# Norm2 in place, more expert weights ahead of the routing, and a shorter routing chain in a two-layer hybrid trunk

## The chip, the cores and the metric

The kernel runs on one core of a Trainium2 chip. The metric is the device time of one execution in microseconds; the median of three executions is compared. The names of the engines in the rows: PE is TensorE (PEld its weight loads), DVE is VectorE, ACT is ScalarE, POOL is GpSimd, and SP is the engine that issues most of the DMAs.

## The reference

Two layers work on 768 tokens of 1024 features (256 of context, 512 of the latent grid). Each layer normalises its input, projects it for four kinds of mixers, joins them, projects the result back and adds it with a gate; then it normalises again (Norm2) and sends every token to two of 32 experts. After the second layer comes a last norm.

```python
def hierarchical_moe(h, w_rg, b_rg, w_re, b_re, w_gu, w_dn):
    g_logits = hf @ w_rg.astype(jnp.float32) + b_rg.astype(jnp.float32)
    _, g_sel = lax.top_k(g_logits, 1)
    p_group = jnp.take_along_axis(jax.nn.softmax(g_logits, axis=-1), g_sel, axis=-1)
...
    w_top, i_top = lax.top_k(jax.nn.softmax(e_in_group, axis=-1), TOP_K)
    w_top = p_group * w_top / jnp.sum(w_top, axis=-1, keepdims=True)
...
    order = jnp.argsort(expert_id)
```

In the second layer only the 512 latent tokens are carried on.

## The kernel before

Tokens lie in tiles of 128 partitions: six tiles in layer 0, four in layer 1 (only the latent ones). A layer runs through its mixers, then the output projection, then the routing, then 16 pairs of experts.

**Projection and Norm2.** The columns of w_out come in four blocks of 256 (`c` = 0 to 3), each in pieces that are loaded (L1485 to L1488) and split on ACT and DVE. `evacuate` takes a tile's projection out of PSUM: tmpo (DVE, L1604), xc (DVE, L1605, which is also stored to XA in DRAM), xh, the row times Norm2's scale (POOL, L1607), and the sum of squares (ACT, L1609). PE turns xc (L1614), the copy xT is made by ACT for c < 3 and by DVE for c = 3 (L1616), and PE multiplies it with the routing weights (po). At c = 3 follow, tile by tile, ss (DVE L1628, POOL L1629 and L1630), xg, the finished Norm2 row with its features put in another order (DVE, L1636, a strided operation), its store to XG in DRAM (SP, L1638), and lg, the logits (DVE, L1639 and L1641).

**Routing.** DVE finds the group and the two experts of each token in steps of a maximum, a comparison and an index: r_m, r_eq, r_ix, r_pen, Ms (L1713 to L1742). The masks go to PE as Am (L1745); from PE's running counts come code, then one-hot rows yes (L1793), and PE multiplies these with MV, which holds token numbers and weights by expert (`by_kind`, L1773, writes it). Out comes row (L1800), the list of tokens of each expert. The softmax weights (r_ex, r_zs, pg, e, gw, gp) and the counts cnt run on DVE between these steps. POOL then gathers rows of XG by the list (L1827, `rows`); PE turns the gathered rows (pt, L1907) and runs the experts.

**Weights of the experts.** A layer has 96 pieces of 1 MB: two of gate and up and one of down for each expert (in_moe_w_gu, in_moe_w_dn). They go through a ring of 18 slots:

```python
SLOTS = ((2, 2, 14), (2, 2, 14))
EARLY = (6, 6)
DEEP = 4
...
        wpre = SLOTS[L][0] + SLOTS[L][1] - PRE
```

The three numbers of a layer are the slots in three pools of memory. The slots of the first two (4) are filled while the projection runs, six more (EARLY) are loaded when the XG writes have been issued, and the rest when the first gather has gone out (`mark`), with at most DEEP = 4 loads under way. SP's queue keeps its order. Between the ring's last piece and the next, SP reads 17 counts (cnti) into registers. From then on a piece is loaded when a pair has used up the one in its slot.

**Norms.** norm1 squares a tile on ACT (L468), makes 1/sqrt by a logarithm and an exponential (L291, L292, with a table load L190), scales the tile on DVE (L476) and lets PE turn it (L487). The last norm does the same without the turn (L2051, L2059).

Of the kernel before, what the change touches and what calls it, by code (L numbers as in the profile page):

```python
# [2095 lines left out]
```

## Time and profile before

| what | value |
|---|---|
| runs | 1787.74, 1791.43, 1797.10 us; median 1791.43 |
| the profiled execution | 1788.17 us, span 1786.4 us, granted TensorE clock 0.928 |
| busy share of the span | PE 83%, DVE 40%, ACT 29%, POOL 20% |
| moved by DMA | 365.87 MB, mean 205 GB/s |

The span is the time from the first instruction to the last; the execution's own time has 1.8 us more around it. The shares are means over stages of very different kinds (mixers, projection, experts), so a stage has to be read by itself. PE takes part in nearly everything; DMA is busy in stretches.

### The profile page before, as it was taken

How to read it: one execution, taken by the hardware profiler on the slowest of the kernel's cores; microseconds unless marked ns; L12 is line 12 of the kernel's file. 1: busy time of each engine (PE TensorE's matmuls, PEld its weight loads, DVE VectorE, ACT ScalarE, POOL GpSimd, SP SyncE). 2: the span in 40 equal slices, each digit the busy share in tenths (PEclk: the TensorE clock that was granted, in tenths of full speed). 3: DMA queues.
4: the chain of work that ended last, by engine and by line, in shares of the span. 5: the costliest groups of instructions: out<-in, count | busy, mean ns of one | idle time of the engine just before them, and what ended most of it. 6: DMA issues, size and time to landing. Idle time of an engine off the chain costs nothing. (4 is left out here: it accounts for less than half of the span.)

```text
span 1786.4 us, 26530 instructions
## 1 busy us (share of the span) xinstructions
PE 1479.2 (83%) x10467; PEld 989.5 (55%) x10467; DVE 709.6 (40%) x1423; ACT 523.5 (29%) x1064; POOL 364.0 (20%) x271
## 2 busy tenths in 40 slices
PE   5999999989889748878885989998787766878783
PEld 3888778746679723322324978676465762322221
DVE  5353353485733561111114352635875262111111
ACT  5242452464423100000004432625643211000001
POOL 0012120120102334635431030301200132111100
PEclk9999989999999869999997999989898888999997
DMA  8342411167447399899994332202443659999994
GB/s 269 107 137 70 123 55 33 36 225 233 145 160 210 118 385 334 303 388 382 371 318 140 92 90 70 73 30 72 145 160 112 182 193 378 376 368 369 380 388 173
DMA packets 182864, 365.87 MB, mean 205 GB/s; under 512 B 42705, under 2 KB 93569, under 8 KB 182401
## 3 DMA queue, kind: packets, MB, share of 16 engines
q1 hardware_dynamic: 172368, 342.11, 54.1%
q0 software_dynamic: 9216, 20.99, 4.7%
q8 instruction: 130, 2.13, 0.5%
q14 instruction: 78, 0.63, 0.1%
q10 hardware_dynamic: 1072, 0.01, 0.0%
HBM read 338.48 MB, written 39.65 MB: 212 GB/s over the span
## 5 line engine op out<-in xcount | busy, mean ns | idle before, releaser
L288 PE MATMUL mm<-w,xT 128*64 128x512 f32 x1072 | 287.5, 624 | 22.5 <-PEq L1993 11.6
L288 PE MATMUL pj<-h,w 128*128 128x256 f32 (+1 forms) x1224 | 227.2, 341 | 0.5 <-DVE u L932 0.3
L288 PEld LDWEIGHTS pj<-h,w 128*128 128x128 f32 x1224 | 189.0, 191 | 28.8 <-issue 5.2
L288 PEld LDWEIGHTS mm<-w,xT 128*64 128x64 f32 x1072 | 88.4, 143 | 189.1 <-issue 158.3
L288 PE MATMUL sc<-w,aT 128*64 128x512 f32 x536 | 136.9, 600 | 18.7 <-ACT aT L1933 17.2
L1923 ACT ACTIVATE ac<-mm 128x256 f32<-128x256 f32 (+1 forms) x35 | 13.4, 383 | 358.0 <-PE mm L288 358.0
L288 PE MATMUL pj<-w,h 128*128 128x256 f32 x864 | 118.1, 294 | 0.0
L1924 DVE TENSOR_TENSOR ac<-ac,mm 128x256 f32<-128x256 f32 (+1 forms) x35 | 14.7, 421 | 253.5 <-ACT ac L1923 253.5
L288 PEld LDWEIGHTS pj<-w,h 128*128 128x128 f32 x864 | 111.3, 199 | 3.8 <-issue 3.1
L1971 POOL DMA_INDIRECT XA<-yes,row x32 | 50.8, 1589 | 300.6 <-DVEq L1993 270.9
L288 PEld LDWEIGHTS sc<-w,aT 128*64 128x64 f32 x536 | 44.4, 136 | 88.3 <-issue 57.2
L288 PE MATMUL mm<-w,h 128*128 128x256 f32 x624 | 83.5, 294 | 11.6 <-PEq L1511 6.4
L518 DVE TENSOR_TENSOR w<-w 128x2048 fp32r<-128x2048 f32 (+1 forms) x26 | 58.0, 2231 | 81.6 <-ACT w L516 81.6
L288 PEld LDWEIGHTS mm<-w,h 128*128 128x128 f32 x624 | 80.2, 201 | 12.2 <-issue 6.6
L1907 PE MATMUL pt<-masks,w 128*128 128x128 f32 x256 | 44.2, 308 | 43.7 <-PEq L1993 25.7
L1907 PEld LDWEIGHTS pt<-masks,w 128*128 128x128 f32 x256 | 30.5, 154 | 89.0 <-issue 77.1
L288 PE MATMUL sc<-h 128*128 128x256 f32 (+3 forms) x144 | 62.2, 551 | 10.7 <-ACT um L1208 9.9
L1607 POOL TENSOR_TENSOR xh<-xc,gr 128x512 f32<-128x512 f32 (+1 forms) x25 | 30.9, 1237 | 195.4 <-DVE xc L1605 132.6
L1954 POOL TENSOR_SCALAR yes<-gate,own 128x1024 f32<-128x1024 f32 (+1 forms) x19 | 60.8, 3199 | 16.9 <-DMA w<-XG,row 13.5
L1908 ACT COPY xT<-pt 128x512 f32<-128x512 f32 x32 | 18.7, 585 | 155.2 <-PE pt L1907 135.7
L516 ACT ACTIVATE w<-w 128x2048 fp32r<-128x2048 f32 (+1 forms) x26 | 48.0, 1848 | 50.7 <-PE pj L288 36.7
L288 PE MATMUL x<-u 64*32 64x32 f32 (+5 forms) x944 | 54.4, 250 | 8.4 <-DVE u L772 8.0
(391 smaller groups left out, 2420.7 us busy)
## 6 DMA issues: line engine op xcount, KB each, us to landing
w<-in_moe_w_gu_dram SPq DMA_DIRECT2D x128, 1024.0 KB
w<-in_moe_w_dn_dram SPq DMA_DIRECT2D x64, 1024.0 KB
w<-in_w_mod_dram SPq DMA_DIRECT2D x40, 1024.0 KB
w<-in_w_in_dram SPq DMA_DIRECT2D x22, 1024.0 KB
wm<-in_w_mod_dram SPq DMA_DIRECT2D x8, 1024.0 KB
XG<-xg SPq DMA_DIRECT2D x10, 512.0 KB
w<-in_w_out_dram SPq DMA_DIRECT2D x8, 512.0 KB
w<-in_w_out_dram SPq DMA_DIRECT2D x16, 256.0 KB
```

The lines of the kernel that those rows point to most:

```text
L288: TE.matmul(o, lhsT, rhs, start=start, stop=stop, **kw)
L516: S.activation(hi[:, :, 0:o], raw[:, :, 0:o], AF.Copy)
L518: V.tensor_tensor(lo[:, :, 0:o], raw[:, :, 0:o], hi[:, :, 0:o].bitcast(F32), op=ALU.subtract)
L1607: G.tensor_tensor(xh[:, t0 - qt0:t0 - qt0 + m, cs], xs, bc(gr[:, 1, w], 0, m), op=ALU.mult)
L1907: TE.transpose(pt[:, u * P:(u + 1) * P], xg[:, o:o + P], ident)
L1908: (V.tensor_copy if g else S.copy)(xT[:, 4 * g:4 * g + 4], pt.rearrange("p (k t) -> p k t", k=4))
L1923: S.activation(ac[rs_], pm[rs_, 0:256], AF.Silu)
L1924: V.tensor_tensor(ac[rs_], ac[rs_], pm[rs_, 256:512], op=ALU.mult)
L1954: G.tensor_scalar(gt[rs_], gate[rs_, 1], own[rs_], None, op0=ALU.mult)
L1971: G.indirect_dma_start(out=XA, out_offset=bass.IndirectOffsetOnAxis(ap=row, axis=0), in_=ye, in_offset=None, bounds_check=T - 1, oob_is_er ...
```

## The change

- **Norm2 in place.** POOL writes xh in the order of features in which XG is read (the write has a stride), the shift row is stored in that order in DRAM by the modulation, and DVE finishes the row in xh itself, without strides and without xg. XG is written from xh. xT is copied by ACT for all c.
- **Slots.** Still 18 per layer, but 7 (layer 0) and 9 (layer 1) in the first two pools instead of 4. So 7 and 9 pieces are loaded during the projection, then six as before, then 5 and 3.
- **Routing.** The routing's tiles (the pool "rout") are opened after the projection's pools are closed. Mp and the first products of MV go from DVE to POOL; the subtraction of gate from POOL to DVE. That subtraction, the weights and the counts are issued only after row. PE's products for the weights and for the second list of rows go behind the first half of pair 0.
- **Norms.** norm1 multiplies by a diagonal (dgn) on PE instead of scaling the tile and turning it; in the branch that runs this concerns layer 1. The table loads are issued ahead of the first square.

```diff
 RING, RING2 = 5, 5
-SLOTS = ((2, 2, 14), (2, 2, 14))
+SLOTS = ((2, 5, 11), (2, 7, 9))
...
                 V.tensor_copy(AB2s[L][:, :, g // 2 - 3, 4 * (g % 2):4 * (g % 2) + 4],
                               pm[:, 0:P].rearrange("p (j c) -> p c j", j=4)[:, 0:2, :])
             if g >= 4:
-                for w in range(2):
+                if g in (6, 7):
+                    mp = cp.tile([P, P], F32, name="mp", tag="mp", bufs=1)
+                    V.tensor_copy(mp.rearrange("p (e q) -> p q e", e=2), mr.rearrange("p (q e) -> p q e", e=2))
+                    for w in range(2):
+                        nc.sync.dma_start(MOD[L][w, 3 * D:4 * D].rearrange("(e i j q) -> i j e q", e=2, i=2, j=4)[g - 6],
+                                          mp.rearrange("(j r) (e q) -> j r e q", r=32, e=2)[:, w])
+                for w in range(2) if g not in (6, 7) else ():
                     nc.sync.dma_start(MOD[L][w, cs].rearrange("(j c) -> j c", j=4),
                                       mr.rearrange("(j r) c -> j r c", r=32)[:, w, :])
...
-                if L and then and n == 0:
-                    ln_exp()
                 rstd_of(ss, ss, D)
+            dgs = {}
+
             def scale(n):
-                x_, ss = sss.pop(n)
-                V.tensor_scalar(xn[n], x_, ss, None, op0=ALU.mult)
+                _, ss = sss.pop(n)
+                dgs[n] = wk.tile([P, P], F32, name="dgn", tag="dgn", bufs=3)
+                V.tensor_scalar(dgs[n], ident, ss, None, op0=ALU.mult)
...
-                        TE.transpose(pt[:, (n - n0) * P:(n - n0 + 1) * P], xn[n][:, k * P:(k + 1) * P], ident)
+                        mm(pt[:, (n - n0) * P:(n - n0 + 1) * P], xn[n][:, k * P:(k + 1) * P], dgs[n], True, True, skip_group_check=True)
...
+            if L and then:
+                ln_exp()
             staged(range(NT), fetch, square, scale, turn)
...
-        wr_ = pr.pool("rout")
...
-        lg = wr_.tile([P, N, 36], F32, name="lg")
+        lg = tabp.tile([P, N, 36], F32, name="lg")
...
-            G.tensor_tensor(xh[:, t0 - qt0:t0 - qt0 + m, cs], xs, bc(gr[:, 1, w], 0, m), op=ALU.mult)
+            pairs = "p n (q e) -> p n q e"
+            G.tensor_tensor(xh[:, t0 - qt0:t0 - qt0 + m].rearrange("p n (e c q) -> p c n q e", e=2, c=4)[:, c],
+                            xs.rearrange(pairs, e=2), bc(gr[:, 1, w], 0, m).rearrange(pairs, e=2), op=ALU.mult)
...
-            (S.copy if c < 3 else V.tensor_copy)(xT[:, 0:m], pt[:, 0:m * 2 * P].rearrange("p (u k t) -> p u k t", u=m, k=2))
+            S.copy(xT[:, 0:m], pt[:, 0:m * 2 * P].rearrange("p (u k t) -> p u k t", u=m, k=2))
...
-                xg = wk.tile([P, D], F32, name="xg", tag="xg", bufs=2)
-                pairs = "p (q e) -> p q e"
-                V.scalar_tensor_tensor(xg.rearrange("p (e q) -> p q e", e=2), xh[:, n - qt0].rearrange(pairs, e=2), ss[:, n:n + 1],
-                                       shift[:, w].rearrange(pairs, e=2), op0=ALU.mult, op1=ALU.add)
-                nc.sync.dma_start(XG[n * P:(n + 1) * P, :], xg)
+                V.scalar_tensor_tensor(xh[:, n - qt0], xh[:, n - qt0], ss[:, n:n + 1], shift[:, w], op0=ALU.mult, op1=ALU.add)
+                nc.sync.dma_start(XG[n * P:(n + 1) * P, :], xh[:, n - qt0])
...
         ph.close()
         ro.close()
         u1.close()
+        wr_ = pr.pool("rout")
         wpools[2] = ew.pool("moew2", side="right")
         yes = wpools[2].tile([P, YE, D], F32, name="yes")
...
             G.memset(t_, 0.0)
         for w in ws:
             row_bcast(gate[:, w], MOD[L][w, 5 * D:6 * D])
-        if not last:
-            G.tensor_tensor(gate[:, 1], gate[:, 1], gate[:, 0], op=ALU.subtract)
         prefetch(EARLY[L])
...
-        V.tensor_tensor(Mp, Ms[:, :, :, 0:16], Ms[:, :, :, 16:32], op=ALU.add)
...
-        by_kind(V, 0, [bc(tok1[:, i, q_], 0, 2) for i in range(2)])
+        G.tensor_tensor(Mp, Ms[:, :, :, 0:16], Ms[:, :, :, 16:32], op=ALU.add)
+        by_kind(G, 0, [bc(tok1[:, i, q_], 0, 2) for i in range(2)])
+        known = []
...
-            V.scalar_tensor_tensor(row, val[:, 0], -1.0, val[:, 1], op0=ALU.add, op1=ALU.add)
+            known.append(V.scalar_tensor_tensor(row, val[:, 0], -1.0, val[:, 1], op0=ALU.add, op1=ALU.add))
...
+        with tc.issue_after(known[0].ins):
+            if not last:
+                V.tensor_tensor(gate[:, 1], gate[:, 1], gate[:, 0], op=ALU.subtract)
+            ex = sm([4], "ex4")
...
+            by_kind(V, 2, in_parts(V, gw, "gp"))
+            V.tensor_scalar(e1, e1, 1873.0, None, op0=ALU.add)
+            V.tensor_copy(cnti, cnt[0:1, 0])
-        slot_weights(ohs, tabs[0])
...
-        def block_in(xg, xT=None):
+        def block_in(xg, xT=None, engs=(S.copy, V.tensor_copy)):
...
-                (V.tensor_copy if g else S.copy)(xT[:, 4 * g:4 * g + 4], pt.rearrange("p (k t) -> p k t", k=4))
+                engs[g](xT[:, 4 * g:4 * g + 4], pt.rearrange("p (k t) -> p k t", k=4))
...
-        slot_weights(slot_table(wk, 1, tabs[1]["row"]), tabs[1])
-        xT = into(0)
+        xT = block_in(xgs[0], None, (S.copy, S.copy))
+            if p_ == 0:
+                slot_weights(ohs, tabs[0])
+                slot_weights(slot_table(wk, 1, tabs[1]["row"]), tabs[1])
...
-        if n == 2:
-            ln_exp()
...
+    ln_exp()
     staged(range(2, NT), square, scale)
```

How the change moves instructions is seen best in the order of each engine. SP in layer 1's projection, from the c = 2 block on; before (rows carry the waits, DMAHW a load or store queue, DMASW a gather queue):

```order
L1450 DMA w_25458<-in_moe_w_gu_dram 128x2x1024 [waits DMAHW2_49]
L1488 DMA w<-in_w_out_dram 128x4x256 [waits DMAHW4_49,DMAHW5_49,DMAHW3_49,DVE_49]
L1555 DMA xc<-XA 128x4x256 [waits DMAHW7_49,DMAHW6_49,PE_49]
L1606 DMA XA<-xc 128x2x256 x2
L306 DMA gr<-MOD_103 128x256 [waits Pool_49]
L306 DMA gr<-MOD_103 128x256 [waits DMAHW0_49]
L1485 DMA w<-in_w_out_dram 128x2x256 [waits DMAHW3_49,DMAHW1_49,DVE_49]
L1486 DMA w<-in_w_out_dram 128x2x256 [waits DMAHW2_49]
L1555 DMA xc<-XA 128x4x256 [waits DMAHW6_49,DMAHW5_49,PE_49]
```

One load of expert weights stands ahead of two pieces of w_out, and none between them. The same stretch of SP now:

```order
L1460 DMA w_25487<-in_moe_w_gu_dram 128x2x1024 [waits DMASW6_49,DMASW4_49,DMAHW2_49,DMASW0_49,PE_49]
L1498 DMA w<-in_w_out_dram 128x4x256 [waits DMAHW4_49,DMAHW5_49,DMAHW3_49,DVE_49]
L1564 DMA xc<-XA 128x4x256 [waits DMAHW7_49,DMAHW6_49,PE_49]
L1465 DMA w_25543<-in_moe_w_dn_dram 128x2x1024
L1495 DMA w<-in_w_out_dram 128x2x256 [waits DMAHW3_49,DVE_49]
L1496 DMA w<-in_w_out_dram 128x2x256
L1615 DMA XA<-xc 128x2x256 [waits DMAHW0_49]
L1615 DMA XA<-xc 128x2x256 [waits DMAHW1_49]
L306 DMA gr<-MOD_103 128x256 [waits DMAHW2_49,Pool_49]
L306 DMA gr<-MOD_103 128x256
L1465 DMA w_25643<-in_moe_w_dn_dram 128x2x1024 [waits DMAHW4_49]
L1564 DMA xc<-XA 128x4x256 [waits DMAHW1_49,DMAHW5_49,DMAHW0_49,PE_49]
```

Two loads of down pieces have come in, one of them right ahead of w_out; three more of gate and up follow within five rows. The load that was there before now waits for PE and three gather queues besides the one queue.

DVE in layer 0 where Norm2 ends and the routing begins; before:

```order
L1713 TENSOR_REDUCE r_m_11853<-lg 128x4 [waits DVE_49]
L1605 TENSOR_TENSOR xc<-xc,tmpo 128x256 [waits DVE_49]
L1636 SCALAR_TENSOR_TENSOR xg<-xh,ss,shift 128x512x2 [waits DMAHW0_49,Pool_49]
L1639 TENSOR_TENSOR lg<-po,ss 128x36 [waits PE_49]
L1616 COPY xT<-pt 128x256 [waits PE_49]
L1641 TENSOR_TENSOR lg<-lg,wb_10849 128x36 [waits DVE_49]
L1628 TENSOR_REDUCE ss<-ssq 128x1 [waits Activation_49]
L1714 TENSOR_TENSOR r_eq_11847<-lg,r_m_11853 128x16
L1715 TENSOR_TENSOR r_eq_11847<-r_eq_11847,iom 128x16 [waits DVE_49]
L1636 SCALAR_TENSOR_TENSOR xg<-xh,ss,shift 128x512x2 [waits DMAHW3_49,Pool_49]
L1639 TENSOR_TENSOR lg<-po,ss 128x36 [waits PE_49]
L1716 TENSOR_REDUCE r_ix<-r_eq_11847 128x4 [waits DVE_49]
```

Steps of the routing (r_m, r_eq, r_ix) stand between the last tiles, and each xg waits for the store of the one before last. The same place of DVE now:

```order
L1646 SCALAR_TENSOR_TENSOR xh<-xh,ss,shift 128x1024 [waits Pool_49]
L1648 TENSOR_TENSOR lg<-po,ss 128x36 [waits PE_49]
L1640 TENSOR_REDUCE ss<-ssq 128x1 [waits Activation_49]
L1650 TENSOR_TENSOR lg<-lg,wb_10862 128x36 [waits DVE_49]
L1646 SCALAR_TENSOR_TENSOR xh<-xh,ss,shift 128x1024 [waits Pool_49]
L1648 TENSOR_TENSOR lg<-po,ss 128x36 [waits PE_49]
L1650 TENSOR_TENSOR lg<-lg,wb_10862 128x36 [waits DVE_49]
L1721 TENSOR_REDUCE r_m_11868<-lg 128x4 [waits DMAHW4_49,DMAHW6_49,DMAHW2_49,DMAHW7_49,DMAHW1_49,DMAHW0_49]
L1721 TENSOR_REDUCE r_m_11868<-lg 128x2 [waits DVE_49]
L1722 TENSOR_TENSOR r_eq_11862<-lg,r_m_11868 128x16 [waits DVE_49]
```

The steps of the routing now all stand behind the last lg, and the first of them waits for six DMA queues. xg has become xh, and the xT copy is gone from DVE.

DVE in layer 0 from the last Am on; before:

```order
L1745 TENSOR_TENSOR Am<-Ms 128x64 [waits DVE_49]
L1755 TENSOR_TENSOR Mp<-Ms 128x192
L1864 RECIPROCAL r_zs<-r_zs 128x6 [waits DVE_49]
L1773 TENSOR_TENSOR MV<-Mp,tok_94 128x192 [waits DVE_49]
L1759 COPY cn<-mm 128x32 [waits PE_49]
L1773 TENSOR_TENSOR MV<-Mp,tok_94 128x192
L1762 TENSOR_SCALAR mo<-cn 128x16 [waits DVE_49]
L1762 TENSOR_SCALAR mo<-cn 128x16
L1866 TENSOR_TENSOR e_11972<-e_11972,r_zs 128x12 [waits Activation_49]
L1882 TENSOR_TENSOR cnt<-cn 128x16
L1885 TENSOR_SCALAR cnt<-cn 128x16
L1867 TENSOR_TENSOR r_zs<-e_11972 128x6 [waits DVE_49]
```

Steps of the weights (r_zs, e) and counts (cnt) stand among those that lead to code. The same place of DVE now, up to row and the gate subtraction:

```order
L1753 TENSOR_TENSOR Am<-Ms 128x64 [waits DVE_49]
L1766 COPY cn<-mm 128x32 [waits PE_49]
L1769 TENSOR_SCALAR mo<-cn 128x16 [waits DVE_49]
L1769 TENSOR_SCALAR mo<-cn 128x16
L1774 TENSOR_TENSOR e_11931<-mm,mo 128x192 [waits DVE_49,Activation_49]
L1781 SCALAR_TENSOR_TENSOR u__11932<-e_11931,u__11932 128x192 [waits DVE_49]
L1782 TENSOR_TENSOR tm_11925<-Ms,u__11932 128x384 [waits DVE_49]
L1783 TENSOR_REDUCE code<-tm_11925 128x12 [waits DVE_49]
L1803 TENSOR_TENSOR yes<-iota_84,code 128x768 [waits DVE_49]
L1803 TENSOR_TENSOR yes<-iota_84,code 128x768
...
L1810 SCALAR_TENSOR_TENSOR row_11944<-val 128x16 [waits DVE_49]
L1863 TENSOR_TENSOR gate<-gate 128x1024 [waits DMAHW3_49,DMAHW2_49]
```

Mp, MV, r_zs, e of the weights and cnt have left the stretch; gate stands behind row, and everything else of the weights behind gate.

## Rows read from the trace of the kernel before

**Rows 1.** Page, slices: DMA share in 40 equal parts of the span, in tenths.

```profile
DMA  8342411167447399899994332202443659999994
```

**Rows 2.** Windows, layer 1: span, busy us of each engine, clock, DMA share, GB/s.

```profile
1420.00:1440.00 20.00, 20.00 (x173) 20.00 (x173) 7.33 (x10) 6.40 (x17) 5.55 (x4) 1.00 0.90 248
1440.00:1460.00 20.00, 15.72 (x126) 14.97 (x124) 11.41 (x21) 4.28 (x13) 6.61 (x10) 0.93 0.32 118
...
1470.00:1490.00 20.00, 7.39 (x56) 4.32 (x57) 10.62 (x62) 2.38 (x4) 4.39 (x6) 0.55 1.03 410
...
1600.00:1700.00 100.00, 79.33 (x314) 27.69 (x316) 13.91 (x22) 7.29 (x16) 14.73 (x11) 0.95 1.01 374
```

**Rows 3.** Windows, layer 0, in the expert stage.

```profile
715.00:723.00 8.00, 6.26 (x18) 1.87 (x18) 2.00 (x4) 0.64 (x2) 3.89 (x2) 1.00 0.07 24
...
735.00:917.00 182.00, 150.18 (x628) 52.96 (x626) 27.92 (x43) 14.68 (x33) 86.23 (x42) 0.98 1.03 380
```

**Rows 4.** Timeline of SP, layer 1: start, us issuing, and what.

```profile
1451.79 0.33 SPq L1638 DMA_DIRECT2D XG<-xg  x1
...
1465.86 1.29 SPq L1455 DMA_DIRECT2D w<-in_moe_w_dn_dram  x2
...
1498.43 3.40 SPq L1455 DMA_DIRECT2D w<-in_moe_w_dn_dram  x2
1512.08 4.16 SPq L1450 DMA_DIRECT2D w<-in_moe_w_gu_dram  x4
```

**Rows 5.** Timeline of DVE, layer 0: first and last tile of c = 3.

```profile
600.90 2.07 DVE L1636 SCALAR_TENSOR_TENSOR xg<-xh,ss,shift 128x1024 f32<-128x1024 f32 x1 [0.97 <-POOL ss L1630]
602.81 0.41 DVE L1616 COPY xT<-pt 128x256 f32<-128x256 f32 x1
...
623.26 2.00 DVE L1636 SCALAR_TENSOR_TENSOR xg<-xh,ss,shift 128x1024 f32<-128x1024 f32 x1 [0.65 <-POOL ss L1630]
```

**Rows 6.** Timeline of DVE, layer 1: first and last tile of c = 3.

```profile
1449.69 2.07 DVE L1636 SCALAR_TENSOR_TENSOR xg<-xh,ss,shift 128x1024 f32<-128x1024 f32 x1 [0.97 <-POOL ss L1630]
...
1462.94 2.01 DVE L1636 SCALAR_TENSOR_TENSOR xg<-xh,ss,shift 128x1024 f32<-128x1024 f32 x1 [0.68 <-POOL ss L1630]
```

**Rows 7.** DMA view of 1440 to 1475 us: GB/s in 40 slices.

```profile
GB/s 331 361 267 66 0 0 0 0 0 150 19 0 0 9 253 366 280 0 0 0 0 332 267 0 295 370 84 0 0 220 346 220 257 206 365 412 426 426 403 440
```

**Rows 8.** Timelines of DVE and ACT in the last norm.

```profile
1776.15 1.28 DVE L2059 SCALAR_TENSOR_TENSOR o<-x,ss,gf 128x1024 f32<-128x1024 f32 x1 [13.70 <-ACT ss L292]
...
1774.29 1.28 ACT L190 ACT_TABLE_LOAD   x1
```

**Rows 9.** Timeline of DVE, layer 0: from the last Am to row.

```profile
631.33 0.22 DVE L1745 TENSOR_TENSOR Am<-Ms 128x64 bf16<-128x64 f32 x1
...
632.82 2.35 DVE L1885 TENSOR_SCALAR cnt<-cn 128x16 f32<-128x16 f32 x1
...
641.41 0.16 DVE L1800 SCALAR_TENSOR_TENSOR row<-val 128x16 int32<-128x16 f32 x1
```

**Rows 10.** Timeline of POOL, layer 0, the same stretch.

```profile
632.69 2.45 POOL L1698 TENSOR_TENSOR gate<-gate 128x1024 f32<-128x1024 f32 x1 [1.25 <-DMA gate<-MOD]
642.49 1.28 POOL L1827 DMA_INDIRECT w<-XG,row  x1 [7.35 <-DMA w<-in_moe_w_gu_dram]
```

**Rows 11.** Timeline of PE, layer 0: products for weights, and pair 0.

```profile
641.64 0.80 PE L288 MATMUL mm<-MV,yes 128*128 128x64 bf16 x12 [2.10 <-DVE row L1800]
...
663.27 0.44 PE L1931 MATMUL po<-masks,ac 128*128 128x128 f32 x2 [1.26 <-DVE ac L1924]
```

**Rows 12.** Timeline of PE, layer 1: first half of pair 0.

```profile
1486.86 7.65 PE L288 MATMUL mm<-w,xT 128*64 128x512 f32 x32
```

**Rows 13.** Timeline of ACT, norm1 of layer 1.

```profile
961.16 1.28 ACT L190 ACT_TABLE_LOAD   x1
```

**Rows 14.** Groups of PE, by form: busy us and mean ns of one.

```profile
L288 PE MATMUL x<-u 128*128 128x128 f32 x80 | 12.8, 289 | 0.0
...
L1614 PE MATMUL pt<-masks,xc 128*128 128x128 f32 x80 | 15.3, 303 | 3.7 <-DVE lg L1639 3.7
```

More of the change, by code (lines that the diff above doesn't have):

```diff
@@ L1849, in layer @@
             rows(p_)
-        ex = sm([4], "ex4")
-        pg = sm([1], "pg")
-        V.tensor_tensor(ex, gl, m0.to_broadcast([P, N, 4]), op=ALU.subtract)
-        S.activation(ex, ex, AF.Exp)
-        V.tensor_reduce(pg, ex, axis=AX.X, op=ALU.add)
-        e2 = wr_.tile([P, 2, N], F32, name="e2")
-        zs = sm([1], "zs")
-        V.tensor_tensor(le2, le, m1.to_broadcast([P, N, 32]), op=ALU.subtract)
-        S.activation(le2, le2, AF.Exp)
-        V.tensor_reduce(zs, le2, axis=AX.X, op=ALU.add)
@@ L1861, in layer @@
-        V.tensor_tensor(m2, m2, m1, op=ALU.subtract)
-        S.activation(e2[:, 1], m2.rearrange("p n o -> p (n o)"), AF.Exp)
-        V.memset(e2[:, 0], 1.0)
-        V.reciprocal(zs, zs)
-        V.reciprocal(pg, pg)
-        V.tensor_tensor(e2, e2, bc(zs.rearrange("p n o -> p (n o)"), 0, 2), op=ALU.mult)
-        V.tensor_tensor(zs.rearrange("p n o -> p (n o)"), e2[:, 0], e2[:, 1], op=ALU.add)
-        V.reciprocal(zs, zs)
-        V.tensor_tensor(zs, zs, pg, op=ALU.mult)
-        gw = wr_.tile([P, 2, N], F32, name="gw")
@@ L1871, in layer @@
-        V.tensor_tensor(gw, e2, bc(zs.rearrange("p n o -> p (n o)"), 0, 2), op=ALU.mult)
-        by_kind(V, 2, in_parts(V, gw, "gp"))
-        slot_weights(ohs, tabs[0])
-        V.tensor_scalar(e1, e1, 1873.0, None, op0=ALU.add)
-        V.tensor_tensor(tm2, Ms, bc(e1, 0, 2), op=ALU.mult)
-        V.tensor_reduce(left, tm2.rearrange("p r n (h a) -> p r n h a", h=2), axis=AX.X, op=ALU.add)
-        V.tensor_scalar(left, left, -2000.0, None, op0=ALU.add)
-        cnt = wr_.tile([P, 2, 17], F32, name="cnt")
@@ L1889, in layer @@
-        V.tensor_scalar(cnt[:, 0, 16:17], cnt[:, 0, 16:17], -128.0, 0.0, op0=ALU.add, op1=ALU.max)
-        cnti = tabp.tile([1, 17], I32, name="cnti")
-        V.tensor_copy(cnti, cnt[0:1, 0])
+        with tc.issue_after(known[0].ins):
+            if not last:
+                V.tensor_tensor(gate[:, 1], gate[:, 1], gate[:, 0], op=ALU.subtract)
+            ex = sm([4], "ex4")
+            pg = sm([1], "pg")
+            V.tensor_tensor(ex, gl, m0.to_broadcast([P, N, 4]), op=ALU.subtract)
+            S.activation(ex, ex, AF.Exp)
+            V.tensor_reduce(pg, ex, axis=AX.X, op=ALU.add)
+            e2 = wr_.tile([P, 2, N], F32, name="e2")
+            zs = sm([1], "zs")
+            V.tensor_tensor(le2, le, m1.to_broadcast([P, N, 32]), op=ALU.subtract)
+            S.activation(le2, le2, AF.Exp)
+            V.tensor_reduce(zs, le2, axis=AX.X, op=ALU.add)
+            V.tensor_tensor(m2, m2, m1, op=ALU.subtract)
+            S.activation(e2[:, 1], m2.rearrange("p n o -> p (n o)"), AF.Exp)
+            V.memset(e2[:, 0], 1.0)
+            V.reciprocal(zs, zs)
+            V.reciprocal(pg, pg)
+            V.tensor_tensor(e2, e2, bc(zs.rearrange("p n o -> p (n o)"), 0, 2), op=ALU.mult)
+            V.tensor_tensor(zs.rearrange("p n o -> p (n o)"), e2[:, 0], e2[:, 1], op=ALU.add)
+            V.reciprocal(zs, zs)
+            V.tensor_tensor(zs, zs, pg, op=ALU.mult)
+            gw = wr_.tile([P, 2, N], F32, name="gw")
+            V.tensor_tensor(gw, e2, bc(zs.rearrange("p n o -> p (n o)"), 0, 2), op=ALU.mult)
+            by_kind(V, 2, in_parts(V, gw, "gp"))
+            V.tensor_scalar(e1, e1, 1873.0, None, op0=ALU.add)
+            V.tensor_tensor(tm2, Ms, bc(e1, 0, 2), op=ALU.mult)
+            V.tensor_reduce(left, tm2.rearrange("p r n (h a) -> p r n h a", h=2), axis=AX.X, op=ALU.add)
+            V.tensor_scalar(left, left, -2000.0, None, op0=ALU.add)
+            cnt = wr_.tile([P, 2, 17], F32, name="cnt")
+            c0_, c1_ = cnt[:, 0, 0:16], cnt[:, 1, 0:16]
+            V.tensor_tensor(c1_, cn[:, 0:16], cn[:, 16:32], op=ALU.add)
+            V.tensor_scalar(c1_, c1_, 128.0, 4.0, op0=ALU.is_gt, op1=ALU.mult)
+            V.scalar_tensor_tensor(c1_, cn[:, 0:16], 64.0, c1_, op0=ALU.is_gt, op1=ALU.add)
+            V.tensor_scalar(c0_, cn[:, 16:32], 64.0, 2.0, op0=ALU.is_gt, op1=ALU.mult)
+            V.tensor_tensor(c0_, c0_, c1_, op=ALU.add)
+            V.tensor_tensor(cn, cn, mo, op=ALU.add)
+            V.tensor_reduce(cnt[:, 0, 16:17], cn, axis=AX.X, op=ALU.max)
+            V.tensor_scalar(cnt[:, 0, 16:17], cnt[:, 0, 16:17], -128.0, 0.0, op0=ALU.add, op1=ALU.max)
+            cnti = tabp.tile([1, 17], I32, name="cnti")
+            V.tensor_copy(cnti, cnt[0:1, 0])
```

8 lines of the change are left out of this document (removed).

## The prediction, made before the changed kernel ran

> **What bounds the kernel now.** I read the page's slices first, then tables by stage, then timelines at the joints. In the slices [rows 1] the DMA digits reach 9 only in two long stretches, the expert stages of the two layers. By stage, layer 1 from 1600 to 1700 us [rows 2] has the DMA engines busy 1.01 of the time, PE 79 of 100 us: there the weight stream, 96 pieces of 1 MB, sets the pace. It is fed from a ring of 18 slots, so the stream's end is set by when it starts and how much was loaded before. The same table shows room ahead of it: from 1440 to 1460 us the share is 0.32 (13.6 of 20 us idle). Layer 0 differs [rows 3]: from 715 to 723 us the share is 0.07 while PE works, so the ring is full and PE is late; only from 735 on is DMA the bound (1.03). In layer 0 what counts is therefore when PE gets its first rows; in layer 1 when the stream can run. The page's sums (PE 83%) mix both and decide nothing.
>
> SP's timeline of layer 1 [rows 4] gives the second joint: the six early pieces start at 1465.86, right behind the last XG write at 1464.97; the ring's last two are issued by 1498.43 + 3.40 = 1501.83; piece 18 only at 1512.08. In the 10.25 us between, SP's program reads the 17 counts into registers.
>
> **Edit 1, Norm2 in place (both layers).** Per tile DVE ran a strided xg of 2.00 to 2.07 us [rows 5, 6]; the new one is contiguous, 128x1024, and the nearest row is the final norm's op of the same kind and size, 1.28 us [rows 8]. Going by that row, the tile's round in the new DVE order is: a small reduction of about 0.2 (Am, 128x64, takes 0.22 [rows 9]), the way over POOL 0.97 (the idle time ahead of the xg at 600.90), 1.28, and lg twice plus tmpo, about 0.8 (an estimate: two of 0.2 and one of the 0.41 of a 128x256 operation; xc runs during POOL's way). That is 3.2 us. Layer 0, six tiles: the first still starts at 600.90, the sixth at 600.90 + 5 x 3.2 = 616.9, end 618.2 against 623.26 + 2.00 = 625.26: -7.1. Layer 1, four tiles: from 1449.69, end 1449.69 + 3 x 3.2 + 1.28 = 1460.6 against 1464.95: -4.4. The xT copies that leave DVE (0.41 each, [rows 5]) are in this. POOL's xh now writes with a stride, which no row of before shows; bounds are no dearer (nothing) and DVE's own ratio of strided to contiguous, 2.00/1.28 = 1.56, on some 0.7 us (+0.4 a tile, +2 in layer 0 if all lay on the path). I take nothing, because POOL's xh runs under DVE's 1.28 and the lg work.
>
> **Edit 2, the tiles of the routing come from memory that the projection frees.** The order shows that the first r_m now waits on six DMA queues: all XG writes must have landed. Before, the last write was hidden behind the routing. Its price is bounded by the GB/s slices [rows 7], 0.875 us each: behind the issue at 1451.79 [rows 4] bytes move until the 17th slice ends at 1454.9, so at most 3.1 us. r_m starts at 618.2 + 0.1 + 3.1 = 621.4 in layer 0 and about 1463.8 in layer 1. From the end of the last xg to the start of the last Am passed 631.33 - 625.26 = 6.1 us [rows 5, 9], in which the routing's 36 steps shared DVE with the last lg and with steps of the weights. The weights' steps go, the few routing steps that had been done before come in: 5.4 us, an estimate between 5 and 6. Am then starts at 626.8 instead of 631.33.
>
> **Edit 3, the chain from Am to row.** Before, 641.41 - 631.33 = 10.1 us [rows 9]. In it a 128x16 cnt operation takes 2.35 us; POOL's gate subtraction (2.45 us, [rows 10]) covers the same time from 632.69. Both leave the chain: gate goes behind row, cnt too. Some fifteen more operations of the weights, about 0.1 us each, go behind row as well. 10.1 - 2.2 - 1.8 = 6.1 us. Row at 632.9, gather 1.1 later as before (642.49 - 641.41), 634.0 against 642.49: **-8.5 us**. Mp and two MV products move to POOL. Their cost there is unknown: nothing if they end during DVE's code and yes work, at most 1.4 us if four POOL operations of 0.35 us each hold DVE. I take nothing, since PE needs MV only after yes. The row shows the two engines standing on each other (2.35 under 2.45). [...]
>
> The weights' small matmuls (36 in layer 0, three runs of 12, the longest 0.80 us [rows 11], together at most 2.4) move behind pair 0's first half. There PE waits 1.26 us for ac [rows 11], which covers part: at most +1.1, I take 0.8. Layer 0 in all: **-7.7**, bounds -3.5 (landing 5 us, POOL and contention in full) and -11. Since PE and the full ring hold until 723, then DMA from a full ring, the shift passes through to the layer's end whole; the three extra preloads of layer 0 give nothing by themselves.
>
> **Edit 4, nine pieces instead of four before the routing in layer 1.** Five pieces leave the stretch that begins with the early loads. At 406 GB/s (1470 to 1490 shows 410, [rows 2]) one takes 2.6 us: -13.0. The stretch itself starts 4.4 us sooner (edit 1). SP then reaches piece 18 at 1512.08 - 17.4 = 1494.7. The slot it takes is free when pair 0's first half ends, 1486.86 + 7.65 = 1494.5 before [rows 12], some 3 earlier after. So SP still sets the time, and the stream, and with it the end, move by **-17.4**. Bounds: -20 if the counts' reading shrinks into the wait, -4.4 if the five pieces only fill time in which something else was waited for. Their cost where they go: 13 us of DMA in 1420 to 1460, where 2 and 13.6 us are idle [rows 2]; w_out's pieces could come up to 2.6 us late. Nothing taken.
>
> **Edit 5, small ones.** Two table loads of 1.28 us [rows 8, 13] go into idle time of ACT ahead of the norms: -2.6. In norm1 of layer 1 the scale becomes a 128x128 diagonal and transposes become products: 48 transposes before, 48 products after. Rows: 128x128 f32 products 289 ns, transposes 303 ns [rows 14]: nothing. [...]
>
> **Sum.** 1788.2 (span 1786.4 and 1.8 around it) - 7.7 - 17.4 - 2.6 = 1760.5. The median of the runs, 1791.4, is 3.3 above that execution, so I give 1761.
>
> **Rivals.**
> A. Layer 1's preloads don't count: something other than SP and DMA (memory of the new slots free late) sets piece 18. Against it stands the idle DMA before 1460; for it, that order puts more waits on the loads. Only -4.4 is left of edit 4: 1774.
> B. The routing gains nothing: the landing takes 8 us instead of 3 since early pieces and gate follow at once, and POOL's strided writes stretch each tile. Edits 1 to 3 fall to nothing in layer 0 (+7.7) and the start of the stretch in layer 1 (+4.4): 1773.
> C. The change doesn't do what it says: the stream in both layers is bound by its total of bytes and the gaps reappear elsewhere (a later idle DMA as in 715 to 723). What is left are the table loads and a few us: 1783.
> D. Slower: a preload that waits for its memory holds the queue. SP issues in order, and behind the new loads stand w_out pieces, xc and XA writes of the projection. If one holds SP until a stage of the projection ends, PE waits for w_out. It decides against the change from 14 us a layer (28 in all); at 20 us a layer the time is 1761 + 40 = 1801. For it: in the order one of layer 1's loads now waits for PE and three gather queues where it waited for one load. Against it: the idle DMA time from 1440 to 1460 says that the projection leaves room for loads that come late.
> [...]
>
> **Chances.** Forecast 0.62, A 0.13, B 0.10, C 0.07, D 0.06, E 0.02. The forecast alone spans 1745 (all upper bounds) to 1770. The range must take A and B in and leaves C, D, E out: 1745 to 1777. A difference under 0.5% (9 us) can hardly be told from none; faster are forecast, A and B, 0.85; same C, 0.07; slower D and E, 0.08.
>
> **What would show it.** Right: xh of 1.3 us per tile, the rounds 3.2 us apart; r_m 3 us behind the last XG issue; row about 6 us behind Am; gather of layer 0 near 634; piece 18 of layer 1 some 26 us sooner than 1512 (17.4, and 7.7 and 1.3 won before it), DMA share near 1 from there on; no table load between square and ss in the last norm. Wrong: waits of PE on w_out in the projection (D); an idle gap of DMA between pieces 17 and 18 of more than 5 us (A); r_m more than 5 us behind the last write or POOL's xh over 1.1 us (B); a final shift of the stream's end that is smaller than that of its start (C).

## The result, and the profile after

The kernel became slower: 1800.43 us median against 1787.29, ratio 1.0066, 95% interval [1.0048, 1.0083]; the forecast was 1761. Each kernel ran 20 times for this comparison. The profiled execution has a span of 1795.5 us against 1786.4. One experiment below (e10) runs in 1768.76 us, ratio 0.9892 [0.9863, 0.9921]. It keeps most of the change, takes back what made it slow, and adds two things that the change did not have: counts read one at a time, which alone make the kernel before 0.9945 of its time (e9), and eight small products on PE (e7).

Cutting both spans at the same seven events shows where it went. All columns are us, differences of starts in one profiled execution each, so a row adds up to its span. e1 to e11 are the experiments below. a: start to the last product of PE that reads um, a tile of layer 0's mixers. b: to the projection's first product. c: to pair 0's first product. d: to the first square of norm1 in layer 1. e: to the first product of layer 1's projection. f: to pair 0's first product there. g: to the end.

| kernel | a | b | c | d | e | f | g |
|---|---|---|---|---|---|---|---|
| before | 516.2 | 5.5 | 131.0 | 307.3 | 429.4 | 97.5 | 299.5 |
| after | 519.1 | 8.8 | 124.9 | 311.3 | 437.3 | 97.5 | 296.6 |
| e1 | 518.7 | 11.2 | 126.2 | 309.6 | 432.3 | 98.3 | 288.3 |
| e2 | 515.1 | 5.4 | 130.7 | 307.2 | 436.4 | 97.6 | 306.0 |
| e3 | 517.6 | 11.0 | 124.8 | 309.0 | 428.2 | 99.1 | 289.9 |
| e4 | 511.8 | 10.5 | 127.5 | 307.7 | 430.5 | 95.7 | 297.1 |
| e6 | 515.9 | 10.9 | 125.1 | 308.5 | 433.2 | 99.1 | 285.5 |
| e7 | 514.8 | 5.5 | 127.5 | 308.2 | 430.2 | 98.8 | 286.2 |
| e8 | 513.8 | 9.6 | 121.7 | 309.7 | 433.5 | 96.6 | 292.2 |
| e9 | 511.2 | 5.6 | 130.8 | 300.7 | 429.2 | 97.1 | 293.9 |
| e10 | 518.5 | 5.6 | 123.6 | 305.3 | 433.5 | 96.6 | 284.9 |
| e11 | 515.0 | 5.5 | 124.1 | 304.8 | 433.5 | 93.7 | 294.5 |

Column a scatters by 8 us between kernels that barely differ there (e3 and e4 are the same up to it), column e by 5 among those without the added table loads, and column g by 4 between e3, e6 and e7, whose programs are the same there; so no cause is read from a few us in these three. From before to after: a +2.9 (scatter), b +3.2, c -6.1, d +4.0, e +7.9, f 0, g -2.9; the sum is +9.1. Part of the predicted gain in layer 0 is there (c), but b takes half of it back and d more than the other half: b, c and d together take 443.8 us before and 445.0 after. The largest loss (e, with norm1 of layer 1) and the smallness of the gain in g (with the last norm) hang on the table loads, which follow first.

**ACT in the last norm** (timeline: start, us, line, operation), against the one load of [rows 8]. Before, the first square on ACT and the last operation of the norm on DVE:

```profile
1773.12 1.06 ACT L2051 ACTIVATE o<-x 128x1024 f32<-128x1024 f32 x1 [15.22 <-DMA x<-XA]
...
1781.44 1.28 DVE L2059 SCALAR_TENSOR_TENSOR o<-x,ss,gf 128x1024 f32<-128x1024 f32 x1 [0.32 <-ACT ss L292]
```

After, ACT:

```profile
1757.10 1.28 ACT L190 ACT_TABLE_LOAD   x1
1772.49 1.28 ACT L2066 ACT_TABLE_LOAD   x1 [14.10 <-DMA x<-XA]
...
1774.95 1.28 ACT L291 ACT_TABLE_LOAD   x1
1776.24 0.29 ACT L291 ACTIVATE ss<-ss,eps 128x1 f32<-128x1 f32 x1
1776.56 1.28 ACT L292 ACT_TABLE_LOAD   x1
1777.85 0.20 ACT L292 ACTIVATE ss<-ss 128x1 f32<-128x1 f32 x1
...
1779.11 1.28 ACT L291 ACT_TABLE_LOAD   x1
1780.40 0.29 ACT L291 ACTIVATE ss<-ss,eps 128x1 f32<-128x1 f32 x1
1780.72 1.28 ACT L292 ACT_TABLE_LOAD   x1
```

L190 is the load ahead that the change moved. It runs at 1757.10, right behind the last pair; then a conditional follows (L2022), the norm's first square loads again (L2066), and from there every Ln (L291) and every Exp (L292) of the four tiles has a load of its own. VectorE's four norm operations show the price:

```profile
1778.08 1.28 DVE L2072 SCALAR_TENSOR_TENSOR o<-x,ss,gf 128x1024 f32<-128x1024 f32 x1 [16.45 <-ACT ss L292]
...
1790.57 1.28 DVE L2072 SCALAR_TENSOR_TENSOR o<-x,ss,gf 128x1024 f32<-128x1024 f32 x1 [2.88 <-ACT ss L292]
```

They stand (1790.57 - 1778.08) / 3 = 4.16 us apart. From the moment the first x is there to the last of them it took 1790.57 - 1772.49 = 18.1 us, before 1781.44 - 1773.12 = 8.3: +9.8. In norm1 of layer 1 the same, against [rows 13]:

```profile
965.22 1.28 ACT L291 ACT_TABLE_LOAD   x1
966.52 0.29 ACT L291 ACTIVATE ss<-ss,eps 128x1 f32<-128x1 f32 x1
...
967.87 1.28 ACT L292 ACT_TABLE_LOAD   x1
...
969.38 1.28 ACT L291 ACT_TABLE_LOAD   x1
...
970.99 1.28 ACT L292 ACT_TABLE_LOAD   x1
...
974.30 1.28 ACT L190 ACT_TABLE_LOAD   x1
```

Here the load that should have been ahead runs behind the first two tiles, and they load four times. From norm1's first square to the last product that turns a tile it took 30.4 us before and 38.8 after; 31.8 in e1, which has one load there again.

**The diagonal in norm1.** The instructions of PE that turn the six tiles of layer 1 (count, then ns min/median/max, first and last start), before and after:

```profile
L487 PE MATMUL mm<-masks,xn x48: 270/273/477, 964.8 to 990.4; 128*128 128x128 f32 x48
```

```profile
L288 PE MATMUL mm<-dgn,xn x96: 273/275/582, 969.8 to 1002.9; 128*128 128x128 f32 x96
```

Each of the 48 products is two matmuls of PE, each as long as one transpose. Little of this shows in the time: the stretch of 30.4 us above became 31.5 to 31.8 us in the kernels with the diagonal and one table load there.

**The weight loads of the next layer.** SP issues the first w_in pieces of layer 1 at 956.70, before at 932.93:

```profile
932.93 1.88 SPq L511 DMA_DIRECT2D w<-in_w_in_dram  x3
```

```profile
956.70 1.86 SPq L521 DMA_DIRECT2D w<-in_w_in_dram  x3
```

**Layer 0's tail and routing**, against [rows 5, 9] (DVE) and [rows 10] (POOL):

```profile
606.96 1.28 DVE L1646 SCALAR_TENSOR_TENSOR xh<-xh,ss,shift 128x1024 f32<-128x1024 f32 x1 [0.97 <-POOL ss L1642]
...
611.92 1.29 DVE L1646 SCALAR_TENSOR_TENSOR xh<-xh,ss,shift 128x1024 f32<-128x1024 f32 x1 [1.60 <-POOL ss L1642]
...
614.86 1.74 DVE L1646 SCALAR_TENSOR_TENSOR xh<-xh,ss,shift 128x1024 f32<-128x1024 f32 x1 [0.71 <-POOL ss L1642]
...
624.94 1.28 DVE L1646 SCALAR_TENSOR_TENSOR xh<-xh,ss,shift 128x1024 f32<-128x1024 f32 x1 [0.78 <-POOL ss L1642]
...
629.72 0.24 DVE L1721 TENSOR_REDUCE r_m<-lg 128x4 f32<-128x16 f32 x2 [3.16 <-DMA XG<-xh]
...
641.88 0.18 DVE L1810 SCALAR_TENSOR_TENSOR row<-val 128x16 int32<-128x16 f32 x1
```

```profile
614.79 0.73 POOL L1618 TENSOR_TENSOR xh<-xc,gr 128x256 f32<-128x256 f32 x1
...
642.36 1.98 POOL L1837 DMA_INDIRECT w<-XG,row  x1 [5.60 <-DVE row L1810]
```

Each in-place operation takes 1.28 us, or 1.74 where POOL's xh runs beside it (614.79 and 614.86); the rounds are (624.94 - 606.96) / 5 = 3.6 us apart on average, and the first is the longest (611.92 - 606.96 = 4.96 us); r_m waits 3.16 us for the XG writes.

**PE at the start of layer 0's projection** (weight loads):

```profile
524.67 0.28 PEld L288 LDWEIGHTS mm<-w,h 128*128 128x128 f32 x1 [5.53 <-ACTq L1521]
527.87 2.43 PEld L288 LDWEIGHTS mm<-w,h 128*128 128x128 f32 x11 [2.91 <-issue]
```

One weight load, then 2.91 us without a wait on anything that the profile shows ("issue").

**Layer 1's stream**, windows against [rows 2], then SP and PE against [rows 4, 12]:

```profile
1440.00:1460.00 20.00, 20.00 (x173) 20.00 (x172) 5.55 (x7) 5.08 (x13) 2.61 (x2) 1.00 0.84 289
...
1480.00:1500.00 20.00, 4.12 (x28) 2.87 (x29) 12.54 (x77) 2.73 (x8) 5.67 (x9) 0.50 1.02 402
1500.00:1520.00 20.00, 18.88 (x108) 7.23 (x108) 3.88 (x16) 2.19 (x4) 2.79 (x3) 0.97 0.67 242
1600.00:1700.00 100.00, 82.95 (x337) 28.57 (x335) 16.29 (x25) 8.04 (x18) 15.76 (x12) 0.97 1.01 372
```

```profile
1473.18 2.72 SPq L1647 DMA_DIRECT2D XG<-xh  x2
...
1492.07 3.58 SPq L1465 DMA_DIRECT2D w<-in_moe_w_dn_dram  x2
1513.81 2.27 SPq L1460 DMA_DIRECT2D w<-in_moe_w_gu_dram  x4
```

```profile
1498.88 8.18 PE L288 MATMUL mm<-w,xT 128*64 128x512 f32 x32
...
1510.02 3.65 PE L288 MATMUL sc<-w,aT 128*64 128x512 f32 x16 [0.46 <-ACT aT L1946]
```

Piece 18 is issued at 1513.81, 0.14 us behind the end of pair 0 (1510.02 + 3.65 = 1513.67), and the DMA engines idle a third of 1500 to 1520 us.

### The profile page after: what moved, and what is told of

It reads as the page before. It is cut to its first block, busy times and chain, and to the rows that moved or that the text cites. A ratio compares the mean times of both kernels' runs of the same rounds, so it can differ in the third digit from the quotient of the medians.

```text
span 1795.5 us, 26666 instructions
## 1 busy us (share of the span) xinstructions
PE 1479.9 (82%) x10515; PEld 999.4 (56%) x10515; DVE 696.1 (39%) x1410; ACT 546.3 (30%) x1089; POOL 361.4 (20%) x276
## 3 DMA queue, kind: packets, MB, share of 16 engines
q8 instruction: 131, 2.15, 0.5%
## 5 line engine op out<-in xcount | busy, mean ns | idle before, releaser
L288 PE MATMUL x<-u 64*32 64x32 f32 (+5 forms) x944 | 54.7, 251 | 11.2 <-DVE u L782 9.3
```

The source lines that it names most:

```text
L288: TE.matmul(o, lhsT, rhs, start=start, stop=stop, **kw)
```

## The experiments

Ratios are to the kernel before, run on the same chip beside it. The times given are medians; a difference by the ratios and one by the medians can be 2 us apart. e1 to e4 ran on one chip, e6 to e11 on another.

**e1_tables_back**: the changed kernel with the two table loads where they were.

```
 S.activation(junk, x_, AF.Square, accum_out=ss)
+if L and then and n == 0:
+    ln_exp()
...
-if L and then:
-    ln_exp()
 staged(range(NT), fetch, square, scale, turn)
...
 fixed(S.activation(o_, xt, AF.Square, accum_out=ss))
+if n == 2:
+    ln_exp()
...
-ln_exp()
 staged(range(2, NT), square, scale)
```

> The changed kernel with the two table loads issued where they were before the change, nothing else undone. Theory T (the loads ahead of the norms are not kept: ACT changes its table for each logarithm and each exponential, 5 loads in norm1 of layer 1 and 9 in the last norm instead of 1 and 1): 15 us less than the changed kernel (5.4 in norm1, 9.8 in the last norm), about 1785 us, ratio to the kernel before 0.999. Rival R (the loss sits in Norm2, the routing or the slots, and the table loads were moved at a gain of 2.6 us): 1803 us, ratio 1.008 or more.

Measured: 1786.4 us, 0.9986 [0.9967, 1.0005], not told apart from the kernel before. One load in each norm again:

```profile
1772.86 1.28 ACT L190 ACT_TABLE_LOAD   x1
1774.16 0.29 ACT L291 ACTIVATE ss<-ss,eps 128x1 f32<-128x1 f32 x1
1774.49 0.20 ACT L292 ACTIVATE ss<-ss 128x1 f32<-128x1 f32 x1
```

1800.4 - 1786.4 = 14 us were the loads (theory T).

**e2_tables_alone**: the kernel before with the same lines moved the other way, and nothing else.

> The kernel before with the move of the two table loads alone. Theory T: 14 to 15 us slower than the kernel before, ratio 1.008, with four table loads between the first square and the third in norm1 of layer 1 and two per tile in the last norm; pairs of the last layer may load tables too. Rival R: 2.6 us faster, ratio 0.9985.

Measured: 1799.4 us, 1.0064 [1.0037, 1.009]: this edit alone loses about 12 us, nearly as much as the whole change. Its excess stands in columns e (+7.0) and g (+6.5); T had 14 to 15.

**e3_l0_slots_back**: e1 with layer 0's three added preloads taken back.

```
-SLOTS = ((2, 5, 11), (2, 7, 9))
+SLOTS = ((2, 2, 14), (2, 7, 9))
```

> Table loads back as in the first run, and layer 0's slots back to 2, 2, 14, layer 1's kept at 2, 7, 9. Theory W (layer 0's larger second pool lies on the memory into which the next layer's first w_in pieces were loaded during the experts, so that these now wait for the last scatters): w_in issued near 933 us again, norm1 4 to 6 us earlier than in the first run, about 1780 us, ratio 0.996. Rival (w_in is late for another reason, or norm1 waits for its tokens anyway): within 1 us of the first run.

Measured: 1780.66 us, 0.9955 [0.9933, 0.9977]. w_in is issued 23 us sooner than in e1 (959.36 there), column e is 4.1 shorter, the time 5.7:

```profile
936.11 1.74 SPq L521 DMA_DIRECT2D w<-in_w_in_dram  x3
```

**e4_slots_back**: e1 with both layers' slots as before, `SLOTS = ((2, 2, 14), (2, 2, 14))`.

> Table loads back and the slots of both layers back to 2, 2, 14: Norm2 in place, the routing and the diagonal alone. Theory G (with nine pieces loaded ahead, piece 18 waits for the end of pair 0, not for SP): with the old slots piece 18 again goes out when SP has read the counts, so the preloads of layer 1 are worth the difference of the two gates, 6 us and not 13: 1786 us, ratio 0.999. Rival (the forecast's sum): 13 us above the third run.

Measured: 1785.2 us, 0.9992 [0.9967, 1.0018], not told apart from the kernel before. Against e3, layer 1's five preloads are worth 4.5 us (6.6 by the ratios), not 13: column g is 7.2 shorter with them, column f 3.4 longer. As G said, piece 18 goes out here as soon as the last count is read (at 1506.57), 8 us behind the end of pair 0 (1498.95):

```profile
1506.93 4.19 SPq L1460 DMA_DIRECT2D w<-in_moe_w_gu_dram  x4
```

**e6_shift_store_back**: e3 with the shift row stored in plain order, and read with a stride in Norm2's operation (the code is shortened).

```
-if g in (6, 7):
-    mp = ...                 # permuted copy, stored in pieces of 64
...
-V.scalar_tensor_tensor(xh[..], xh[..], ss[:, n:n + 1], shift[:, w], ...)
+V.scalar_tensor_tensor(xh[..] (e q), xh[..] (e q), ss[:, n:n + 1], shift[:, w] (q e -> e q), ...)
```

> e3 with one piece of the change taken back: the shift row is stored in its plain order again (no permuted copy, no stores of 64-element pieces), and Norm2's in-place operation reads it with a stride instead. All kernels with the change lose about 3 us between 406 and 431 us of layer 0's span. Theory S (the permuted store makes SP and VectorE late there): that loss goes, 3 us, and the strided read costs at most 0.75 us a tile, 6 tiles in layer 0 and 4 in layer 1, of which part is hidden: ratio to before 0.994 to 0.997, and the last product on um before the projection ends 2 to 3 us earlier against e3. Rival (those 3 us come from elsewhere, e.g. the order of the w_mod loads): that product ends where e3 has it, ratio 0.9955 to 0.999.

Measured: 1779.22 us, 0.9944 [0.9922, 0.9966]; the last product on um at 515.89. That lies inside the scatter of column a (e4 and e8, which store as e3 does, have 511.8 and 513.8). Theory S is not borne out: the loss that I had read between 406 and 431 us can't be told from the spread between executions.

**e7_pe_pad**: e3 with eight transposes of 32x32 ahead of layer 0's branch.

```
+if L == 0:
+    pd = ppt()
+    for _ in range(8):
+        TE.transpose(pd[0:32, 0:32], ident[0:32, 0:32], ident[0:32, 0:32])
 strong = nc.values_load(fi[0:1, 0:1], min_val=0, max_val=1000)
```

> e3 plus 8 transposes of 32x32 on PE ahead of the branch into layer 0's projection; nothing else. Theory F (PE's program comes in blocks of 16 KB; in the changed kernel the branch lands at the end of a block, so that PE runs one weight load and then waits for a second block: 3.2 to 5.6 us from the first LDWEIGHTS to the first MATMUL, where before has 0.03): the target moves into the next block, the first MATMUL follows its LDWEIGHTS at once, idle time ahead of the projection's first product falls from 10.7 us to 5 to 7, and the time falls by 3 to 5 us against e3, ratio to before 0.993. Rival (the gap is a wait that the records don't show, for an operand): the gap stays, ratio 0.9955 to 0.9965.

Measured: 1780.44 us, 0.9961 [0.9942, 0.998]. The gap is gone; the weight loads run on at once:

```profile
520.28 2.00 PEld L288 LDWEIGHTS mm<-w,h 128*128 128x128 f32 x9 [4.98 <-ACTq L1525]
```

Column b falls from 11.0 to 5.5, as expected; column c takes 2.7 back, and the time does not resolve the rest. F's gap is gone with the pad as it forecast; the gain in time is not shown. Its 16 KB is the size of the packets of queue q8 (16.4 KB, last section); no run shows where in one the branch lands.

**e8_rout_early**: e3 with the routing's pool opened ahead of the projection.

```
 pr, ph = pools(), pools()
+wr_ = pr.pool("rout")
...
 u1.close()
-wr_ = pr.pool("rout")
```

> e3 with the routing's small tiles in a pool opened ahead of the projection, as before the change, so that they don't take memory which the XG writes still read. Theory L (the first r_m waits for the XG writes to land, 3.16 us in layer 0 and 2.91 in layer 1, and this wait is on the path): the wait goes, pair 0 starts 3 us earlier in each layer, time 4 to 6 us below e3, ratio 0.992 to 0.993. Rival (the gather must wait for the same landing anyway, or DVE has the last lg to do): only 0 to 2 us, ratio 0.9945 to 0.9955.

Measured: 1780.1 us, 0.9966 [0.9944, 0.9988]. In the trace the wait is gone (r_m starts at 619.23, ahead of the last tile), column c is 3.1 and column f 2.5 shorter than in e3; the whole time is not. Columns e and g of this execution are longer, e within its scatter. Inconclusive as to the time.

**e9_counts_late**: the kernel before, with the counts read one at a time.

```
-cregs = [nc.values_load(cnti[0:1, p_:p_ + 1], min_val=0, max_val=T) for p_ in range(NP + 1)]
...
-with tc.If(cregs[p_] > 0):
+creg = nc.values_load(cnti[0:1, p_:p_ + 1], min_val=0, max_val=T)
+with tc.If(creg > 0):
```

> The kernel before, with one thing changed: the 17 counts are no longer read into registers in one row ahead of pair 0 (10 us on SP), but one at a time just ahead of each pair's conditional. Theory C (in the kernel before it is SP's reading that holds piece 18 of layer 1 at 1512.08, while its slot is free when pair 0 ends at 1501.4): piece 18 starts near 1502, the stream and the end come about 10 us sooner: ratio 0.9945. Rival G (the slot's memory or the pairs themselves hold the stream, the reading is hidden): ratio 0.998 to 1.001. A cost of its own could be a read ahead of each conditional, 0.6 us on each engine: up to 10 us a layer if it lies on the path, ratio 1.000 to 1.005.

Measured: 1777.52 us, 0.9945 [0.9921, 0.997]: C's size. SP no longer pauses for 10 us between pieces 17 and 18, but 1492.78 - (1486.42 + 3.39) = 2.97 us:

```profile
1486.42 3.39 SPq L1455 DMA_DIRECT2D w<-in_moe_w_dn_dram  x2
1492.78 10.73 SPq L1450 DMA_DIRECT2D w<-in_moe_w_gu_dram  x4
```

Only half of it can be layer 1 (column g -5.6, little above that column's scatter); the other half is layer 0 (column d -6.6), where I had not looked for it.

**e10_all**: e3 with the edits of e7, e8 and e9 together.

> e3 with three things together: the 8 small transposes ahead of layer 0's projection, the routing's pool opened ahead of the projection, and the counts read one at a time. Theory: in the traces the fetch gap is worth 3 us (from the last product of the mixing to pair 0's first product of layer 0: 133.0 against 135.8), the landing wait about 4 in layer 0 and 2 in layer 1, the late counts 6 in layer 0 and nothing in layer 1, where in e3 not SP but the end of pair 0 sets piece 18 (1504.98 against 1504.84). Sum -15 against e3: 1766, ratio 0.987; piece 18 of layer 1 again within 1 us behind the end of pair 0. Rival (the parts overlap, since from pair 0 on the stream sets the end): -6 to -9 against e3, ratio 0.991 to 0.992.

Measured: 1768.76 us, 0.9892 [0.9863, 0.9921], 11.9 below e3's median (11 by the ratios), between the theory's 15 and the rival's 6 to 9. Columns b (-5.4), d (-3.7) and f (-2.5) each give a part; c (-1.2), e (+5.3) and g (-5.0) move by about their scatter. Piece 18 again waits for the end of pair 0 (1494.93 + 3.65 = 1498.58):

```profile
1479.18 3.79 SPq L1465 DMA_DIRECT2D w<-in_moe_w_dn_dram  x2
1498.71 2.12 SPq L1460 DMA_DIRECT2D w<-in_moe_w_gu_dram  x4
```

```profile
1494.93 3.65 PE L288 MATMUL sc<-w,aT 128*64 128x512 f32 x16 [0.46 <-ACT aT L1950]
```

**e11_all_slots_back**: e10 with `SLOTS = ((2, 2, 14), (2, 2, 14))`.

> e10 with the five added preloads of layer 1 taken back as well (four pieces ahead of the routing, as in the kernel before). Theory G (the end of pair 0 sets piece 18, so preloads beyond what the DMA engines can load between the last XG write and that end are worth nothing, and they slow the projection: it takes 68.6 us with nine pieces and 64.4 with four): the projection is 4 us shorter and piece 18 still stands at the end of pair 0, with DMA busy all the way: 1762 to 1766, ratio 0.985 to 0.987, no slower than e10. Rival P (the prediction's price: five pieces of 2.6 us leave the stretch that sets the end): 13 us slower than e10, ratio 0.994; half of it if the projection's 4 us come back: 0.992.

Measured: 1775.77 us, 0.9942 [0.9922, 0.9962]: 7.0 us slower than e10 (8.9 by the ratios). Theory G falls; P's half price, 6.5, is the nearest. The windows of e10 and then of e11 show both sides of it:

```profile
1480.00:1500.00 20.00, 17.73 (x96) 7.59 (x98) 3.87 (x16) 3.80 (x6) 2.26 (x3) 0.83 0.79 296
```

```profile
1480.00:1500.00 20.00, 18.89 (x115) 7.73 (x112) 4.07 (x17) 1.72 (x4) 2.60 (x2) 1.00 1.03 395
```

With five preloads more the DMA engines idle 4.2 of these 20 us, until pair 0 ends; with five fewer they never idle, but have 13 us more to move. 13 less the idle 4.2 and the projection's 2.9 (column f, 96.6 against 93.7) is 5.9; the columns give (93.7 + 294.5) - (96.6 + 284.9) = 6.7, the medians 7.0.

## Why the prediction was wrong

**The step that failed** first and by most is edit 5, "Two table loads of 1.28 us [...] go into idle time of ACT ahead of the norms: -2.6". It cost 14 us (e1) or 12 (e2) instead: a term of the wrong sign, as large as the whole loss. The prediction priced the load by its duration and took for granted that the loaded set would still be there when the first Ln came. It was not: in the last norm the first square loaded again, and then every Ln and every Exp. It never looked at ACT's order of instructions, where the loads stand; the orders on record with it are of SP and DVE. In the last norm of after, L190's load (1757.10 us) runs ahead of the conditional, and the first ACT instruction behind it loads again (1772.49). That the set loaded for the square lacks Ln, and the one loaded for Ln lacks Exp, is argued from the loads at 1774.95 and 1776.56; that the conditional is the reason is argued too, as no run takes it away. Why the load in norm1 moved behind two tiles (974.30) is open.

This term alone does not explain the miss: without it the kernel is at 0.9986 (e1), far from 1761. The runs split the forecast of -27.7 us as follows (differences of medians, then of ratios times 1787.5, in us):

| term | forecast | medians | ratios | from |
|---|---|---|---|---|
| table loads moved | -2.6 | +14.0 | +14.3 | after, e1 |
| layer 0's three preloads | 0 | +5.7 | +5.5 | e1, e3 |
| layer 1's five preloads | -13.0 | -4.5 | -6.6 | e3, e4 |
| the rest: edits 1 to 3 and the diagonal | -12.1 | -2.6 | -1.4 | e4, before |

**"The three extra preloads of layer 0 give nothing by themselves."** They cost: e1 to e3 is 5.7 us. What the traces show with them is w_in of layer 1 issued at 957 to 959 us (after, e1), and at 924 to 936 in all other kernels; that this is the cause fits column e of e1 and e3, but its scatter is as large, so the mechanism is argued. Rival D had the right kind of thing (preloads that hold up a load of something else) at the wrong place.

**Edit 4, -17.4.** The step "The slot it takes is free when pair 0's first half ends", and with it "So SP still sets the time", failed: piece 18 follows the end of pair 0 in after (1513.81 behind 1513.67), e3 (1504.98 behind 1504.84) and e10 (1498.71 behind 1498.58). The code suggests why, though no run tests it: behind the pair stands the conditional block with the swapped experts, which may read the same weights again, so that only behind it is the slot free. In the kernel before, SP did set the time: pair 0 ended at 1501.27, and piece 18 followed the last count. The five preloads, priced at 13.0, are worth 4.5 (e3 against e4) and 7.0 (e10 against e11): part goes to DMA engines that wait for that slot, part to the projection, which takes 3 us longer beside them (column f). I had that cost at "nothing taken". Rival A named the place, the memory of the slots, but took the preloads to be worth nothing and kept the 4.4 of the start, which did not come.

**Layer 0's chain, -7.7**, was nearly right step by step, but little of it came through. Column c is -6.1 in after. Landing took 3.16 and 2.91 us against 3.1 forecast; from the last xh's end to Am 8.7 against 8.6; Am to row 6.9 (two Am now, the last at 634.95) against 6.1 (a sum that took 1.8 us for fifteen operations of 0.1). The tail gained less: rounds of 3.6 us instead of 3.2. Most of that is the first round, 4.96 us, in which POOL did two xh ahead of ss and DVE waited 1.60 for it; three of the six operations also took 1.74 instead of 1.28 beside POOL's xh. But c starts later by the gap on PE (b), and when e7 removes that gap, c takes 2.7 us back. Only b, c and d together can be compared: 443.8 us before, 445.0 in after, 445.7 in e4, and 441.2 in e7, so without the gap -2.6 reaches the layer's end. The step "the shift passes through to the layer's end whole" therefore failed as well. One thing that holds the layer up behind pair 0 is shown on the kernel before: with counts read one at a time column d falls by 6.6 (e9).

POOL's strided writes cost nothing (0.73 to 0.75 us each, before 0.72 to 0.74), so rival B's mechanism is out, though layer 0 gained hardly more than the nothing that it forecast. The step "48 products after [...]: nothing" was wrong: they are 96 matmuls of 275 ns against 48 transposes of 273. The rows of 289 and 303 ns gave the time of one matmul and not how many a product needs. The chance of 0.02 for E, slower through the diagonal, has no run behind it: the trace shows two matmuls a product, and about 1 us of them on the path. The contention that layer 0's bound takes in full shows in the xh operations, 1.74 us beside POOL's xh against 1.28 without it. The moved products ended on POOL at 636.75, before DVE had code and yes, and cost nothing visible.

**Layer 1's start, -4.4**, came to nothing in after (column f 97.5 and 97.5): with four preloads it is -1.8 (e4), and the nine take that back (-1.8 in e4 against +1.6 in e3).

**Not in the prediction at all**: the gap on PE, 3 to 5 us at the start of layer 0's projection (below).
